# Two layers of a transformer with modulation on one core: Modulation's sums two products later in a pair with a third buffer, four places for context results, drains by copies, and a fixed order for the keys of layer 1

## The chip, the cores and the metric

The kernel runs on one core of a Trainium2 chip. A core has TensorE (PE, matmuls, with its weight loads PEld), VectorE (DVE), ScalarE (ACT), GpSimd (POOL), and a queue SP from which transfers between the chip's memory and the core's are issued, in order. [...] The metric is device time in microseconds, from one launch.

## The reference, cut to what matters

```python
for layer in range(2):                       # D = 1024, 1024 latent and 256 context positions
    mod_l = (silu(c) @ ada_w[layer] + ada_b[layer]).reshape(batch, 1, 6, D)
    mod_c = (silu(c_ctx) @ ada_w[layer] + ada_b[layer]).reshape(1, 1, 6, D)
    h_l = modulate(x, norm1_g[layer], mod_l, 0)       # rms_norm(x) * (1 + scale) + shift
    h_c = modulate(ctx, norm1_g[layer], mod_c, 0)
    y_c, y_l = ab_mixer(...) if layer == 0 else c_mixer(...)
    x = x + mod_l[:, :, 2] * y_l
    x = x + mod_l[:, :, 5] * mlp(modulate(x, norm2_g[layer], mod_l, 3))   # square(relu(h @ w1)) @ w2
    if layer == 0:
        ctx = ctx + mod_c[:, :, 2] * y_c
        ctx = ctx + mod_c[:, :, 5] * mlp(modulate(ctx, norm2_g[layer], mod_c, 3))
return x
```

The mixer of layer 0 joins a recurrent part with gates and an attention over a window; that of layer 1 is a full attention of 8 query heads over 2 heads of keys and values, whose queries and keys are normalised and rotated. The hidden width of the feed-forward part (mlp) is 4096.

## The kernel before

Data lie transposed: 128 features on the partitions, positions along a row. Each float32 operand is split in a high part and the rest (ACT copies the high part, POOL or DVE subtracts), and a product is three matmuls: high by high, high by rest, rest by high.

The feed-forward part handles the latent positions in two groups of 512 and the weights in blocks of 2 x 2, and gets their four products from seven (sums of operands are multiplied, results are sums of products). `mlp_hidden` goes through 16 pairs of hidden blocks (pairs 0 and 1 in `start`, the rest in `pair(b, A, nxt)`). A pair is seven products of 12 matmuls of 512 columns (`prod`, all at L569): 11 by B11, S1 by T1, 12 by B21, S2 by T2, 22 by T4, S3 by T3, S4 by B22. In layer 0 come 48 matmuls of 256 columns for the context (`direct`), 24 behind the third product and 24 behind the sixth. Banks 0 to 6 take products in turn, bank 7 what fills in. DVE adds the products up in temporaries of the tag "u" (`temp()`, L623), ten places in turn; ACT squares (`finish`, L581 and L582), SP stores the results. At the end of a pair stand the column sums (`column_sums`), in the next one behind S1 the row sums (`row_sums`). Two of the later pairs also do the sums of pairs 0 and 1 (`late_load`).

`filler` puts Modulation of layer 1 in layer 0's pairs: 12 blocks of 512 columns (`ada_sums`). A block has eight loads of 128 x 512 numbers (tag "raw", L202), which DVE multiplies by a number per partition and adds up (L209 the first, L211 the others), for blocks 0 to 3 in two streams (latent, context; the second stream in two halves), for the rest in one. Then matmuls by ones (L220) add over the partitions, and DVE copies the result with the bias (L223). The accumulators have one place each, so the next block begins when L220 is done. In `pair`, `fill` takes one of three steps of a block at three places: loads and updates 0 to 3, loads and updates 4 to 7, L220 and L223.

`mlp_out` then multiplies by the second weights, again in seven products (m1 to m7), two at a time in banks 0 to 3 and 4 to 7, over the hidden blocks. At the end of a group of products `drain` adds the four banks to x: directly by DVE (L1002), or by an ACT copy into a buffer "y" (L1013) and a later addition from there (`flush`). Splits of the next operands (L378 on ACT, L379 on DVE) run beside it.

Layer 1's keys and values (`keys`, `vals`) and the first queries (`project`) follow. A key's squares (L441, L447) are added over the partitions by a matmul with ones (L475), the queries' by L1812. In the attention DVE folds the maxima of a block of scores (L1842, L1845), PE transposes them (L1869); POOL subtracts in `weigh` (L1907). At its end the other mixer outputs are split (`split_mix`, L379) and multiplied (`out`).

The order of instructions on each engine is set by a scheduler that goes by priority, which is the order of the code, and by what waits for what; inside `manual_schedule` it is that of the code. Matmuls of `pair` are written out in the code's order, and DVE's instructions of sums are put where buffers and priority allow.

## Time and profile before

| | |
|---|---|
| median of 3 runs | 2917.3 us (2915.07 to 2924.1) |
| profiled execution | 2912.01 us, span 2910.2 us |
| mean granted clock of TensorE | 0.977 of full speed |
| busy: PE, DVE, ACT, POOL | 2753.9, 1994.1, 1497.0, 1145.2 us |
| loads and stores | 432.10 MB, 148 GB/s over the span |

The span is from the first to the last instruction of the profiled execution; its time as a run has 1.8 us beside it. [...] Busy PE at a clock of 0.50 counts as busy.

### The profile page before, as it was taken

Reading aid. Unit: us, or ns where it says so; the run is one execution under the profiler, and the core shown is the slowest. Engines: PE = TensorE matmul, PEld = TensorE weight load, DVE = VectorE, ACT = ScalarE, POOL = GpSimd, SP = SyncE. Lnnn points to the kernel's source line nnn. Section 1 sums busy time; section 2 is a strip of 40 time slices with the busy share of each in tenths; the row PEclk is TensorE's granted clock in tenths of the full one; section 3 lists DMA queues with packets and bytes.
Section 4 is the critical chain, followed back from the end, with each engine's and each line's share of the span. In section 5 each row is a group of like instructions: output and inputs, shape, how many; then the busy total and the mean of one; then the engine's idle time right before and its main releaser. Section 6 shows DMA issues by size and latency. Waiting matters only on the chain.

```text
span 2910.2 us, 41857 instructions
## 1 busy us (share of the span) xinstructions
PE 2753.9 (95%) x15174; PEld 2344.9 (81%) x15174; DVE 1994.1 (69%) x3296; ACT 1497.0 (51%) x2628; POOL 1145.2 (39%) x757
## 2 busy tenths in 40 slices
PE   6799999999999999999999998999989999999999
PEld 3678788878787777778878897999987888888877
DVE  5836555667867876766777845888886567756665
ACT  5655554444654233343435645888875555544332
POOL 3431220110227455560000653777765298840000
PEclk9999999999999998999999999999999999999999
DMA  6213233352324456569764740000017245577664
GB/s 229 60 49 102 78 101 130 120 194 73 121 84 141 151 188 202 187 225 346 245 215 151 255 151 30 21 25 26 19 62 229 88 140 196 192 250 275 214 228 146
DMA packets 200367, 432.10 MB, mean 148 GB/s; under 512 B 21216, under 2 KB 46944, under 8 KB 200160
## 3 DMA queue, kind: packets, MB, share of 16 engines
q1 hardware_dynamic: 200160, 429.43, 44.4%
q8 instruction: 119, 1.95, 0.3%
q14 instruction: 88, 0.72, 0.1%
HBM read 326.85 MB, written 102.50 MB: 148 GB/s over the span
## 4 chain that ended last, share of the span: by engine, by line
PE 62%; DVE 9%; DMA 6%; issue 6%; POOL 3%; ACT 3%; SPq 0%; DVEq 0%; POOLq 0%; ACTq 0%
PE psum L569 15%; PE psum L997 15%; PE psum L404 4%; PE psum L406 4%; PE psum L405 4%; PE psum L1895 4%; DMA hhiraw<-in_w 3%; PE psum L2080 3%; PE psum L1801 3%; PE psum L1090 2%; POOL W L379 2%; DVE W L379 2%; DMA F<-in_ada_w 1%; PE psum L1421 1%; DVE F L623 1%
## 5 line engine op out<-in xcount | busy, mean ns | idle before, releaser
L379 POOL TENSOR_TENSOR W<-F,W 128x512 fp32r<-128x512 f32 (+2 forms) x323 | 513.5, 1606 | 560.7 <-ACT W L378 435.5
L997 PE MATMUL psum<-W,W 128*128 128x512 f32 x2688 | 617.4, 391 | 11.3 <-DVE x L1002 8.2
L997 PEld LDWEIGHTS psum<-W,W 128*128 128x128 f32 x2688 | 506.2, 189 | 122.0 <-DVE x L1002 9.0
L569 PE MATMUL psum<-hhi,W 128*128 128x512 f32 (+1 forms) x1600 | 442.8, 358 | 9.6 <-ACT F L581 8.7
L378 ACT ACTIVATE W<-F 128x512 fp32r<-128x512 f32 (+2 forms) x380 | 274.7, 738 | 257.4 <-POOL F L542 103.4
L569 PEld LDWEIGHTS psum<-hhi,W 128*128 128x128 f32 x1600 | 287.3, 190 | 55.7 <-ACT F L581 9.7
L569 PE MATMUL psum<-hlo,W 128*128 128x512 f32 (+1 forms) x800 | 286.0, 357 | 0.0
L378 ACT ACTIVATE W<-hhiraw 128x1024 fp32r<-128x1024 f32 x98 | 104.0, 1062 | 331.9 <-PE psum L997 252.8
L404 PE MATMUL psum<-hhi,W 128*128 128x512 f32 (+1 forms) x624 | 232.2, 372 | 2.6 <-ACT F L179 1.4
L406 PE MATMUL psum<-hhi,W 128*128 128x512 f32 (+1 forms) x624 | 228.5, 366 | 1.3 <-POOL W L379 1.3
L405 PE MATMUL psum<-hlo,W 128*128 128x512 f32 (+1 forms) x624 | 228.0, 365 | 0.0
L923 DVE TENSOR_TENSOR hhiraw<-hhiraw 128x512 f32<-128x512 f32 x154 | 105.0, 688 | 125.1 <-DMA hhiraw<-in_w 124.1
L372 POOL TENSOR_TENSOR hlo<-F,hhi 128x512 fp32r<-128x512 f32 (+1 forms) x28 | 35.0, 1254 | 359.0 <-ACT F L371 354.2
L542 POOL TENSOR_TENSOR F<-F 128x512 f32<-128x512 f32 x112 | 169.4, 1513 | 9.9 <-DMA F<-in_w 2.6
L569 PEld LDWEIGHTS psum<-hlo,W 128*128 128x128 f32 x800 | 152.5, 191 | 22.3 <-issue 0.2
L379 DVE TENSOR_TENSOR W<-hhiraw,W 128x1024 fp32r<-128x1024 f32 x98 | 119.5, 1220 | 48.6 <-ACT W L378 48.6
L404 PEld LDWEIGHTS psum<-hhi,W 128*128 128x128 f32 x624 | 118.7, 190 | 25.0 <-ACT F L1353 2.8
L581 ACT ACTIVATE F<-F 128x512 f32<-128x512 f32 x84 | 52.5, 625 | 161.4 <-DVE F L623 161.3
L406 PEld LDWEIGHTS psum<-hhi,W 128*128 128x128 f32 x624 | 118.4, 190 | 20.3 <-POOL W L379 1.7
L405 PEld LDWEIGHTS psum<-hlo,W 128*128 128x128 f32 x624 | 118.9, 191 | 16.7 <-issue 1.4
L569 PE MATMUL psum<-x,W 128*128 128x512 f32 x504 | 123.7, 389 | 0.0
L379 DVE TENSOR_TENSOR W<-hloraw,W 128x1024 fp32r<-128x1024 f32 x98 | 119.3, 1218 | 0.0
(426 smaller groups left out, 6540.7 us busy)
## 6 DMA issues: line engine op xcount, KB each, us to landing
F<-in_w SPq DMA_DIRECT2D x104, 512.0 KB, 4.3
hloraw<-hd SPq DMA_DIRECT2D x90, 512.0 KB, 4.8
hd<-F SPq DMA_DIRECT2D x144, 256.0 KB, 2.2
hhiraw<-in_w SPq DMA_DIRECT2D x72, 512.0 KB, 3.9
hhiraw<-in_w SPq DMA_DIRECT2D x116, 256.0 KB, 5.1
F<-in_ada_w SPq DMA_DIRECT2D x96, 256.0 KB, 3.0
hd<-x SPq DMA_DIRECT2D x88, 256.0 KB, 2.3
F<-in_win SPq DMA_DIRECT2D x33, 512.0 KB, 3.7
```

The costliest lines, as they stand in the source:

```text
L378: nc.scalar.activation(hi, src, AF.Copy)
L379: eng.tensor_tensor(lo, src, hi.bitcast(F32), op=ALU.subtract)
L404: nc.tensor.matmul(ps, sh, mh, start=i == 0, stop=False)
L405: nc.tensor.matmul(ps, sh, ml, start=False, stop=False)
L406: nc.tensor.matmul(ps, sl, mh, start=False, stop=i == n - 1)
L542: add = lambda o, p, q, how: nc.gpsimd.tensor_tensor(o, p, q, op=how)
L569: nc.tensor.matmul(ps, w[i][:, p], B[j][k], start=first and j == 0 and m == 0, stop=last and j == 3 and m == 2)
L923: tt = lambda o, p, q, how: eng.tensor_tensor(o, p, q, op=how)
L997: nc.tensor.matmul(bank(base + i), A[u][:, p], B[v], start=first and m == 0, stop=last and m == 2)
L1801: nc.tensor.matmul(ps, s[:, c], m[:, j, t0 : t0 + QT], start=j == 0 and i == 0, stop=j == ND - 1 and i == 2)
L1895: nc.tensor.matmul(u.o[:, :QT], v[x], p[y], start=c == 0 and m == 0, stop=c == 2 * NB - 1 and m == 2)
L2080: self.nc.tensor.matmul(ps, x[:, c], y, start=first and m == 0, stop=last and m == 2)
```

## The change

Seven edits. In `pair`, the step with L220 stands behind the third product instead of behind the first, and the three steps begin one pair earlier; `fp` gets a third place "raw", taken from the places "u" in layer 0. In `start`, `direct` puts the context's results into the four places "kept" instead of the one place "uc". In `mlp_out`, products with a single use (m6, m7) are drained by copies, except in the last group; the second row of the context's products takes banks 0, 2, 5, 6 instead of 3, 4, 5, 6. Layer 1's keys become one generator for each head, with two buffers for the squares, additions and splits of latent keys on POOL, in an order written out, with the values' chunks between. At the end of attention three splits move from DVE to POOL. In `qk_first` (layer 0) a multiplication by the rotation's cosines stands behind the squares and copies.

```diff
@@ qk_first
-        nc.vector.tensor_tensor(t[:, :n], ps[:, :n], gc[:, l0 : l0 + n], op=ALU.mult)
         nc.scalar.activation(sq[:, :n], ps[:, :n], AF.Square)
...
+        nc.vector.tensor_tensor(t[:, :n], ps[:, :n], gc[:, l0 : l0 + n], op=ALU.mult)
@@ mlp_hidden
+        kept, rest = (cuts(F, H, *(o + i * H for i in range(n))) for o, n in ((3 * PG, 4), (7 * PG, 2)))
         fp = Area()
-        fp.place("raw", cuts(F, H, 5 * PG + H, 6 * PG))
+        fp.place("raw", cuts(F, H, 5 * PG + H, 6 * PG) + (rest[1:] if ctx else []))
...
-            finish(ps, tp.tile([P, CTX], F32, tag="uc"), hc[b][:, e * CTX : e * CTX + CTX])
+            finish(ps, tp.tile([P, CTX], F32, tag=tag), hc[b][:, e * CTX : e * CTX + CTX])
...
-                        direct(f, A[f // 2][2 * (f % 2) : 2 * (f % 2) + 2], g)
+                        direct(f, A[f // 2][2 * (f % 2) : 2 * (f % 2) + 2], g, "kept")
...
-            tp.place("u", kept + rest + [c for t in spare for c in cuts(t, H, 0, H)])
+            tp.place("u", kept + rest[: 1 if ctx else 2] + [c for t in spare for c in cuts(t, H, 0, H)])
@@ pair
-            def fill(last=False):
-                if filler and b > 2 + last:
+            def fill(k):
+
+                if filler and b > k:
                     next(filler(fp, psp, "N"), None)
...
-            fill(True)
             step()
             ps = bank()
             prod(ps, A["S1"], T1)
...
             prod(ps, A["12"], B21)
+            fill(2)
             tt(h11, ps, t)
             finish(h11, h11, part(b, 5))
+            fill(1)
             for g in ctx:
                 direct(f0, (A["11"], A["12"]), g)
-            fill()
...
             tt(t, t, ps, ALU.subtract)
-            fill()
+            fill(1)
@@ mlp_out
-                        drain(base, to[m], final or len(to[m]) == 1, now, done.get(m, ()))
+                        drain(base, to[m], final, now, done.get(m, ()))
...
-        for row, banks in enumerate(((4, 5, 6, 7), (3, 4, 5, 6))):
+        for row, banks in enumerate(((4, 5, 6, 7), (0, 2, 5, 6))):
@@ layer 1
+        def keys(g, kv):
...
+            ps = self.proj(psp, "A", wk[kv], t0, n)
+            yield
+            tile = lambda tag, bufs=1: kp[kv].tile([P, H], F32, tag=tag, bufs=bufs)[:, :n]
+            sq = tile("qsq", 2)
+            nc.scalar.activation(sq, ps[:, :n], AF.Square)
...
+                nc.gpsimd.tensor_tensor(t, t, sw, op=ALU.add)
+            yield
+            ss = psp.tile("Q")
+            nc.tensor.matmul(ss[:, :n], self.ones, sq, start=True, stop=True)
...
+            self.split(*K, rs, nc.vector if vv else nc.gpsimd)
+            yield
...
+        with self.tc.manual_schedule(engines=engines):
+            for x in ks[0]:
+                next(x)
+            for g in range(1, 3):
+                for kv in range(NKV):
+                    next(ks[g][kv])
+                    next(ks[g - 1][kv])
+                    next(ks[g][kv])
+            vals(TGS[1], (0,))
+            next(ks[2][0])
+            vals(TGS[1], (1,))
+            next(ks[2][1])
...
-                    split_mix(CTX, j, stage[j])
+                    split_mix(CTX, j, stage[j], nc.gpsimd)
...
+        with self.tc.manual_schedule(engines=engines):
+            load_q(0)
+            vals(TGS[1], (2, 3))
+            load_q(1)
+            for k in range(2):
+                st = project(k)
+                run(st, 9)
+                vals(TGS[2], (k,))
+                run(st, 99)
```

Where instructions stand, on PE in the pair loop, at a block of sums with one stream. Before, L220 (ones by the accumulator F) stands between the first product and S1 (operands hidA and hb):

```order
L569 MATMUL psum<-hlo,W_4615 128x512
L569 MATMUL psum<-hhi,W_4615 128x512
L220 MATMUL psum<-ones,F 128x2 x4
L569 MATMUL psum<-hidA,W_4615 128x512
L569 MATMUL psum<-hb,W_4615 128x512
L569 MATMUL psum<-hidA,W_4615 128x512 x2
L569 MATMUL psum<-hb,W_4615 128x512
```

In the changed kernel, at the end of the third product and the first matmuls of the context:

```order
L569 MATMUL psum<-hhi,W_4614 128x512
L569 MATMUL psum<-hlo,W_4614 128x512
L569 MATMUL psum<-hhi,W_4614 128x512 x2
L569 MATMUL psum<-hlo,W_4614 128x512
L569 MATMUL psum<-hhi,W_4614 128x512 x2
L569 MATMUL psum<-hlo,W_4614 128x512
L569 MATMUL psum<-hhi,W_4614 128x512 x2
L569 MATMUL psum<-hlo,W_4614 128x512
L569 MATMUL psum<-hhi,W_4614 128x512
L220 MATMUL psum<-ones,F 128x2 x4
L569 MATMUL psum<-hhi,W_4612 128x256
```

L220 moved behind S1 and behind the product of 12 by B21.

On DVE in the same loop, between the last update of one block with two streams and the start of the next (L623 are the pair's additions, a psum among the operands is a product being taken up). Before:

```order
L623 TENSOR_TENSOR F<-psum,F 128x512
L623 TENSOR_TENSOR x_7148<-psum,F 128x512
L623 TENSOR_TENSOR x_7149<-F,x_7148 128x512
L623 TENSOR_TENSOR x_7149<-x_7148 128x512
L623 TENSOR_TENSOR F<-F,x_7148 128x512
L623 TENSOR_TENSOR F<-psum,F 128x512
L623 TENSOR_TENSOR F<-F,x_7148 128x512
L223 TENSOR_TENSOR mod_81<-psum,vec 128x4 x2
L623 TENSOR_TENSOR F<-x_7148,F 128x512
L209 TENSOR_SCALAR F<-F,cs 128x512
L209 TENSOR_SCALAR x_7148<-F,cs 128x256
L209 TENSOR_SCALAR x_7149<-F,cs 128x256
```

In the changed kernel:

```order
L623 TENSOR_TENSOR F<-psum,x_7149 128x512
L623 TENSOR_TENSOR F<-x_7148,F 128x512
L623 TENSOR_TENSOR x_7149<-psum,x_7149 128x512
L623 TENSOR_TENSOR F<-F 128x512
L623 TENSOR_TENSOR x_7148<-x_7148,F 128x512
L623 TENSOR_TENSOR x_7148<-x_7149,F 128x512
L623 TENSOR_TENSOR x_7148<-psum,F 128x512
L623 TENSOR_TENSOR x_7149<-F,x_7149 128x512
L209 TENSOR_SCALAR F<-F,cs 128x512
L223 TENSOR_TENSOR mod_81<-psum,vec 128x4 x2
L209 TENSOR_SCALAR x_7148<-F,cs 128x256
L209 TENSOR_SCALAR x_7149<-F,cs 128x256
```

The same kind of additions stand between two blocks; L223 now stands behind the first operation of the block, and the two operations for the second stream behind it.

In the queue SP, at a block with one stream in pair 7 (L202 loads Modulation's weights, L534 those of the pairs, L584 stores squares: hd of the third product, hc of the context; L605 loads for the late sums). Before:

```order
L202 DMA F<-in_ada_w 128x512 x2
L605 DMA F<-hd_0_6496 128x512
L202 DMA F<-in_ada_w 128x512 x2
L584 DMA hd_7_6503<-x_7148 128x512
L202 DMA F<-in_ada_w 128x512
L584 DMA hc_7_6519<-F 128x256
L202 DMA F<-in_ada_w 128x512
L534 DMA F<-in_w 128x1024
L202 DMA F<-in_ada_w 128x512 x2
L534 DMA F<-in_w 128x1024
```

In the changed kernel:

```order
L202 DMA F<-in_ada_w 128x512 x2
L584 DMA hd_7_6503<-F 128x512
L202 DMA F<-in_ada_w 128x512
L584 DMA hc_7_6519<-F 128x256
L202 DMA F<-in_ada_w 128x512 x2
L534 DMA F<-in_w 128x1024
L202 DMA F<-in_ada_w 128x512 x3
L534 DMA F<-in_w 128x1024
```

Before, five of the eight loads stood ahead of the store of hc_7; now it is three, and three instead of two stand behind the first L534.

On PE at the keys of the context, layer 1 (L1801 a values' chunk, L475 the sums of squares). Before:

```order
L1801 MATMUL psum<-hhi,W_4614 128x256
L475 MATMUL psum<-F,ones 128x256
L1801 MATMUL psum<-hhi,W_4614 128x256
L1801 MATMUL psum<-hlo,W_4614 128x256
L1801 MATMUL psum<-hhi,W_4614 128x256 x2
L1801 MATMUL psum<-hlo,W_4614 128x256
L1801 MATMUL psum<-hhi,W_4614 128x256
L475 MATMUL psum<-F,ones 128x256
L1801 MATMUL psum<-hhi,W_4614 128x256
```

In the changed kernel (L1741 the sum of squares, L404 to L406 the values' chunks):

```order
L404 MATMUL psum<-W_104,hhi 128x256
L405 MATMUL psum<-W_104,hhi 128x256
L406 MATMUL psum<-W_104,hlo 128x256
L404 MATMUL psum<-W_103,hhi 128x256
L1741 MATMUL psum<-F,ones 128x256
L404 MATMUL psum<-W_103,hhi 128x256
L405 MATMUL psum<-W_103,hhi 128x256
L406 MATMUL psum<-W_103,hlo 128x256
```

The two sums of squares stood 7 matmuls apart, in one chunk; now they stand 43 matmuls apart (the other isn't shown), among chunks of values for latent positions.

## Rows read from the trace of the kernel before

**Rows 1.** The page, part 1: engines, busy time, share of the span, instructions.

```profile
PE 2753.9 (95%) x15174; PEld 2344.9 (81%) x15174; DVE 1994.1 (69%) x3296; ACT 1497.0 (51%) x2628; POOL 1145.2 (39%) x757
```

**Rows 2.** Waits of PE, whole span: us in total, times, longest us.

```profile
PE psum L220 <- DVE F L211: 29.4, 8, 7.1
...
PE psum L1205 <- ACT x L1193: 8.1, 1, 8.1
```

**Rows 3.** Windows: us, busy time of each engine, granted clock, DMA share, GB/s.

```profile
966.00:1002.80 36.80, 30.02 (x149) 25.91 (x150) 28.32 (x41) 12.23 (x25) 18.06 (x13) 0.87 0.46 152
...
912.10:1276.70 364.60, 335.20 (x1713) 288.12 (x1711) 264.28 (x322) 128.96 (x250) 212.31 (x144) 0.93 0.55 181
```

**Rows 4.** Timeline of DVE, pairs 4 and 5: start, us, engine, line, operation.

```profile
963.95 0.88 DVE L211 SCALAR_TENSOR_TENSOR x<-F,cs,x 128x256 f32<-128x256 f32 x2
...
973.80 1.17 DVE L623 TENSOR_TENSOR F<-F,x 128x512 f32<-128x512 f32 x1 [3.81 <-ACT F L582]
...
976.60 1.51 DVE L209 TENSOR_SCALAR F<-F,cs 128x512 f32<-128x512 f32 x1
...
999.27 0.87 DVE L211 SCALAR_TENSOR_TENSOR x<-F,cs,x 128x256 f32<-128x256 f32 x2
```

**Rows 5.** Groups of DVE by form, 912.1 to 1276.7: busy us, mean ns.

```profile
L211 DVE SCALAR_TENSOR_TENSOR F<-F,cs 128x512 f32<-128x512 f32 x78 | 72.4, 928 | 42.1 <-DMA F<-in_ada_w 41.8
...
L623 DVE TENSOR_TENSOR F<-psum,F 128x512 f32<-128x512 f32 x43 | 28.6, 679 | 0.5
...
L623 DVE TENSOR_TENSOR F<-F 128x512 f32<-128x512 f32 x20 | 26.2, 1312 | 2.5 <-ACT F L582 2.4
```

**Rows 6.** Waits of DVE, 1035.9 to 1276.7 (pairs with one stream).

```profile
DVE F L211 <- DMA F<-in_ada_w: 33.8, 35, 2.0
```

**Rows 7.** Waits of the queue SP, 870 to 1040.

```profile
SPq L202 <- DVE x L211: 39.2, 22, 3.7
```

**Rows 8.** The page, part 6: DMA issues, KB each, median us to landing.

```profile
F<-in_ada_w SPq DMA_DIRECT2D x96, 256.0 KB, 3.0
...
hd<-F SPq DMA_DIRECT2D x144, 256.0 KB, 2.2
```

**Rows 9.** Timeline of PE at five waits: the bracket names wait and releaser.

```profile
895.50 0.39 PE L569 MATMUL psum<-hhi,W 128*128 128x256 f32 x1 [1.79 <-ACT F L581]
...
1483.19 7.11 PE L997 MATMUL psum<-W,W 128*128 128x512 f32 x20 [4.12 <-DVE x L1002]
...
1669.41 1.82 PE L1090 MATMUL psum<-hb,W 128*128 128x256 f32 x13 [1.65 <-DVE x L1097]
...
2176.62 0.41 PE L1869 MATMUL psum<-ident,F 128*128 128x128 f32 x2 [3.93 <-DVE F L1845]
...
2819.49 6.75 PE L997 MATMUL psum<-W,W 128*128 128x512 f32 x22 [4.06 <-DVE x L1002]
```

**Rows 10.** Timeline of DVE before two of these waits.

```profile
1481.26 1.22 DVE L379 TENSOR_TENSOR W<-hloraw,W 128x1024 fp32r<-128x1024 f32 x1
...
1482.39 2.72 DVE L1002 SCALAR_TENSOR_TENSOR x<-psum,mod,x 128x512 f32<-128x512 f32 x4
...
2168.52 3.10 DVE L379 TENSOR_TENSOR hlo<-F,hhi 128x512 fp32r<-128x512 f32 x3 [0.65 <-ACT hhi L378]
...
2174.77 1.71 DVE L1845 TENSOR_TENSOR F<-F 128x256 f32<-128x256 f32 x1
```

**Rows 11.** Timeline of POOL, end of attention.

```profile
2166.90 2.96 POOL L1907 TENSOR_TENSOR W<-x,W 128x1280 fp32r<-128x1280 f32 x1 [2.17 <-ACT x L1906]
2173.31 2.89 POOL L1907 TENSOR_TENSOR x<-x,x 128x1280 fp32r<-128x1280 f32 x1 [3.45 <-ACT x L1906]
```

**Rows 12.** Waits of PE, 1730 to 1806 (keys and first queries, layer 1).

```profile
PE psum L475 <- ACT F L441: 3.3, 2, 2.5
PE psum L1812 <- ACT F L1809: 3.2, 2, 1.9
PE psum L475 <- ACT F L447: 3.0, 2, 2.8
```

More of the change, by code (lines that the diff above doesn't have):

```diff
@@ L509, in mlp_hidden @@
         tp.place("s", cuts(F, H, 5 * PG))
+        kept, rest = (cuts(F, H, *(o + i * H for i in range(n))) for o, n in ((3 * PG, 4), (7 * PG, 2)))
         fp = Area()
-        fp.place("raw", cuts(F, H, 5 * PG + H, 6 * PG))
+        fp.place("raw", cuts(F, H, 5 * PG + H, 6 * PG) + (rest[1:] if ctx else []))
         fp.place("acc0", cuts(F, H, 6 * PG + H))
-        kept, rest = (cuts(F, H, *(o + i * H for i in range(n))) for o, n in ((3 * PG, 4), (7 * PG, 2)))
         tp.place("kept", kept)
@@ L1748, in vals @@
                 self.split(*V, ps[:, :256], nc.vector)
-        ks = [keys(g) for g in TGS]
+        ks = [[keys(g, kv) for kv in range(NKV)] for g in TGS]
         for _ in range(ND):
             next(side)
-        next(ks[0])
+        for x in ks[0]:
+            next(x)
         next(side)
-        vals(TGS[0])
+        vals(TGS[0], range(4))
         for _ in side:
@@ L1761, in mixer1 @@
         VC = vc[:, :PG].rearrange("p (s c d) -> p s c d", s=2, c=2)
-        next(ks[0])
-        next(ks[1])
-        next(ks[2])
-        next(ks[1])
-        next(ks[2])
+        E = mybir.EngineType
+        engines = {E.PE, E.DVE, E.Activation, E.Pool}
+        with self.tc.manual_schedule(engines=engines):
+            for x in ks[0]:
+                next(x)
+            for g in range(1, 3):
[7 more added lines that the diff above has]
+            next(ks[2][1])
         qtab = self.rope_tables(self.area(PG, 3 * PG), a["rope1"], V_CQ, V_CQS, "rt")
@@ L1925, in load_mix, with split_mix @@
             nc.sync.dma_start(m, mixd[j][:, t0 - CTX : t0 - CTX + 512])
-        def split_mix(t0, j, m):
-            self.split(self.hhi[:, j, t0 : t0 + 512], self.hlo[:, j, t0 : t0 + 512], m, nc.vector)
+        def split_mix(t0, j, m, eng=nc.vector):
+            self.split(self.hhi[:, j, t0 : t0 + 512], self.hlo[:, j, t0 : t0 + 512], m, eng)
         raw = cuts(self.F, PG, 0, PG)
@@ L1986, in early @@
                 out(3, range(ND))
-        for h in range(2):
-            load_q(h)
-        for k in range(2):
-            vals(TGS[1 + k])
-            run(project(k), 99)
+        with self.tc.manual_schedule(engines=engines):
[7 more added lines that the diff above has]
+                run(st, 99)
         psp = self.banks(A=(0,), O=(1,), S=(3, 4, 5, 6, 7))
         ACC, S = (self.psum[:, b * 512 : e * 512] for b, e in ((2, 3), (3, 8)))
-        E = mybir.EngineType
         us = {}
@@ L2002, in on @@
                 f(us[k], *a)
-        with self.tc.manual_schedule(engines={E.PE, E.DVE, E.Activation, E.Pool}):
+        with self.tc.manual_schedule(engines=engines):
             for k in range(NU + 2):
```

27 lines of the change are left out of this document (17 added, 10 removed).

## Prediction

> **What bounds the kernel now.** TensorE (PE) works for 2753.9 of the 2910.2 us of the span [rows 1]; so I read the waits of PE, the largest first, then the stretch of each. The largest is that of the matmuls at L220, which add up Modulation's sums over the partitions, for VectorE's (DVE's) last update at L211: 29.4 us in 8 waits [rows 2], all in the pair loop of layer 0. From the product S1 of pair 3 to that of pair 15 are 12 pairs in 364.6 us, with PE at a mean granted clock of 0.93 [rows 3]; 7% of 364.6 is 25.5 us lost to stretches at the lower level. Waits and clock make 54.9 us; without both a pair would take (364.6 - 54.9) / 12 = 25.8 us. The loop loses 25.5 / 29.4 = 0.87 us to the clock for each us of wait; I use that ratio below.
>
> Why PE waits there is seen on DVE [rows 4]. The last update of one block of sums ends at 963.95 + 0.88 = 964.83; the first operation of the next (L209) starts at 976.60, 11.8 us later, because the pair's other additions stand between, one of which waits 3.81 us for ScalarE (ACT). The block then lasts until 999.27 + 0.87 = 1000.14, 23.5 us. One round on DVE is 35.3 us where PE needs 25.8; in the pair of 966.0 to 1002.8 DVE is busy 28.32 of 36.80 [rows 3], so most of it is work, not waiting. Blocks 0 to 3 carry two streams (24 operations), blocks 4 to 11 one stream (8). In the pairs of the latter DVE waits 33.8 us in 35 waits for the loads of Modulation's weights [rows 6].
>
> **The sums.** The change removes none of them. It moves L220 of a block behind two more products, starts the blocks one pair earlier, and gives their loads a third buffer, whose place it takes from the temporaries (nine instead of ten). A pair holds 84 matmuls of 512 columns and 48 of 256, as much as 108 of 512, so a product of 12 is 25.8 x 12 / 108 = 2.9 us, and the move gives 5.7 us of cover, once. On DVE the order now is: the additions of the pair, the copy L223, then the block with only four or five additions in it.
> Two-stream rounds: the block falls from 23.5 to some 22.5 us, no more, since in SP's queue the stores of the pair's first results, which wait for ACT, still stand among its loads; of the 11.8 us between blocks I keep 11, since the additions that wait for squares stay. That is 33.5 us against 26.7 for PE (25.8 and the 8 matmuls of L220, some 0.9). Block 0 is done beside pair 2; block 1 starts in step with PE, 1 us behind its L220, and is 26.7 - 23.5 = 3.2 us early; block 2 comes 33.5 - 26.7 - 3.2 = 3.6 us late, block 3 another 6.8: 10.4 us.
> One-stream rounds: a load lands in 3.0 us [rows 8] and an update takes 0.93 [rows 5]. With two buffers there is one update each (3.0 + 0.93) / 2 = 2.0 us, 16 us a block; with three 1.3 us, 10.5, and I add 2 for the stores among the loads. With 11 between, a round falls from 27 to 23.5, under 25.8, so PE should wait no more, but for two pairs that do the sums of the first two pairs as well: five additions of 1.31 us [rows 5], 6.5 us, of which the 2.3 to spare in this and the pair before take up 4.6. Some 2 us each, 4 in all.
> So 14.4 us of waits stay, with the clock 14.4 x 1.87 = 27: the gain is 54.9 - 27 = **28**. Bounds: 5 us of waits left give 45.5, 20 give 17.5.
>
> **Drains by copies.** At the change from the second to the third group of output products of layer 0, PE waits 4.12 us for DVE [rows 9], which reaches the four drains only at 1482.39, behind other work [rows 10]; ACT copies now free the banks. That would give 4.12 x 1.87 = 7.7. But the split that ends at 1481.26 + 1.22 = 1482.48 [rows 10] makes an operand of the next step, which PE would reach 12 matmuls (2.7 us) after the drain that it no longer waits for, at 1479.07 + 2.7 = 1481.8: 0.7 us of wait, and about as much at the following step, since the four additions now stand ahead of its split. So **5.5** (4 to 7.7). In layer 1 the like wait is 4.06 us [rows 9]; there the splits come earlier: **5** (4 to 7.6).
>
> **Keys of layer 1.** Of the waits in this stretch [rows 12], 3.3 and 3.0 us are of the sum of squares for ACT and 3.2 of the queries' for ACT, of which the shorter, 1.3, stays. In the new order at least 24 matmuls of 512 or 48 of 256 columns stand between a key's projection and its sum of squares, 5.7 us that cover the activations. Taken away: 9.5 - 1.3 = 8.2, and some clock: **9** (4 to 14 with the clock's ratio on all; below if POOL, which takes the additions and splits, comes late for the first scores).
>
> **End of attention.** PE waits 3.93 us [rows 9] for L1845 on DVE, ahead of which three subtractions take 3.10 [rows 10]. They go to GpSimd (POOL). There 128x1280 takes 2.96 us and ends at 2169.86 [rows 11], so 128x512 takes some 1.2, and three end at 2173.4. PE's three outputs that need them now end at 2176.62 - 3.93 = 2172.69, 1.07 us behind DVE's subtractions (2168.52 + 3.10); then near 2174.5, 2.1 us before L1845's result is taken up now: **2** (-0.5 to 5.5).
> The low end comes from this. L1845 reads two operands in SBUF, took 1.71 us, and ended at 2176.48 [rows 10], just after POOL's operation had ended at 2176.20 [rows 11]; an addition with one operand in PSUM takes 0.68 us, with both in SBUF 1.31 in the mean [rows 5].
> [...]
> I take 2 because DVE, freed of 3.10 us, should issue L1845 before POOL starts that operation.
>
> **The rest.** Four places for the context's results take away a wait of 1.79 us [rows 9] but not those beside it: **1** (0 to 3). Other banks for the context's second row take away 1.65 us [rows 9], unless the first keys wait for bank 0: **1.5** (0 to 2). In layer 0 the multiplication moved behind the squares changes the order of many instructions near a wait of 8.1 us for the gates [rows 2]; it may come earlier or later: **0** (-5 to 5).
>
> **Sum.** 28 + 5.5 + 5 + 9 + 2 + 1 + 1.5 = 52 us. The durations are of one execution of 2912.0 us, 5.3 below the median of the three runs, 2917.3; taken from the median the sum gives **2865**.
>
> **Rivals.**
> The loop's waits go altogether: the rounds on DVE get so short that two-stream blocks keep pace. For it: DVE waits 3.81 us in a round for ACT [rows 4], which could vanish when DVE runs late. Against it: 28.32 us of work [rows 3] where PE needs 26.7. Gain of the loop 50, 22 more: **2843**.
> The third buffer does nothing: SP issues all transfers in one order, and its loads already wait 39.2 us in 22 waits for DVE [rows 7]; if other waits in the queue hold the load of the third buffer as well, rounds stay at 35.3 and 27 us. Then block 1 is 26.7 - 24.5 = 2.2 us early, blocks 2 and 3 come 6.4 and 8.6 late, and eight one-stream rounds (27 for 26.2, with the 4 matmuls of L220) wait 0.8 each: 21.4 us, with the clock 40. The loop gains 15, 13 less: **2878**. For it speaks the queue's order: in pair 7 three of the eight loads now stand ahead of the context's store, before it was five. Against it: PE needs the block two products later too, and waits only if that, too, is used up.
> Slower: the place that the loads take away. With nine places for temporaries, the third result of a pair (h11) goes where the pair before had v, which the row sums have just rewritten and SP must store: a store lands in 2.2 us [rows 8]. Between stand L223 and four updates, some 5 us on DVE in a one-stream pair. DVE, and then PE, waits only if the store goes out 2.8 us late; it stands in the queue near loads that wait up to 3.7 us each [rows 7]. At x us a pair over 13 pairs beyond what the round has to spare, the loop changes by 13x - 54.9, and the rest gains 24; it is slower by 0.3% (8.8 us) from x = 6.7 on, at 7 us **2929**. Against it: that takes four such waits in a row, in each pair.
>
> **How the numbers follow.** 0.3% (9 us) is about what a measurement tells from no change. My forecast: 0.52. All waits of the loop gone: 0.17. Third buffer idle: 0.2. Slower: 0.03. The remaining 0.08 are cases in which another edit costs some 20 us of the gain (the start of layer 0, the keys): from 2885 on, or with the buffer idle within 0.3%. The likeliest alone spans 2852 to 2876; 2841 to 2889 reaches over the first two rivals and the lower bound of the loop's gain, 17.5, with that of other terms, and leaves out 0.15. Faster by over 0.3%: 0.95, within: 0.02, slower: 0.03.
>
> **What would show it.** Waits of L220 below 15 us and a clock of 0.96 or more in the loop, in the pairs of blocks 2 and 3 and in the two with the late sums, would show the sums right; waits at all pairs, the idle buffer; waits of DVE for a store, the slower case. No wait over 1.5 us for L1003 (the former L1002) shows the drains, none over 1 us at the keys' sums of squares the order of the keys, L1845 ending before 2175 the end of attention. The forecast is wrong if PE waits elsewhere for what DVE, now denser, does later, above all for its drains of the banks in pairs 2 to 5.

## The result, and the profile after

The changed kernel takes 2882.4 us (2880.9 to 2886.6, four executions) where the kernel before took 2916.2 (2913.8 to 2924.1) beside it: ratio 0.9882, 95% interval 0.9860 to 0.9904. That is 34 us gained where 52 were forecast. The profiled execution has a span of 2881.0 us, 29.2 less than before.

The page's busy times show that the work is the same [rows 1]; PE does its 15174 matmuls in 8.6 us less because less of them falls into stretches at a granted clock of 0.50 (69 us where it was 96, by windows of 2 us that are at 0.50 throughout; mean granted clock 0.981, before 0.977):

```profile
PE 2745.3 (95%) x15174; PEld 2334.7 (81%) x15174; DVE 1992.4 (69%) x3285; ACT 1503.1 (52%) x2640; POOL 1160.9 (40%) x768
```

The waits of PE, as in [rows 2] (us in total, times, longest). L220 fell from 29.4 us to 7.4; a new line is the output products' (L998):

```profile
PE psum L220 <- DVE F L211: 7.4, 5, 3.8
...
PE psum L998 <- DVE W L379: 6.4, 13, 0.9
...
PE psum L1830 <- DVE F L1744: 4.6, 1, 4.6
...
PE psum L998 <- ACT W L378: 2.9, 1, 2.9
...
PE psum L1927 <- DVE F L1892: 2.9, 1, 2.9
```

The windows of the 12 pairs of [rows 3], from S1 of pair 3 to S1 of pair 15, and of the beginning of the output products (us, busy times, granted clock, DMA share, GB/s):

```profile
902.90:1242.40 339.50, 323.47 (x1714) 279.30 (x1713) 263.84 (x324) 130.46 (x254) 215.79 (x145) 0.97 0.59 194
```

```profile
1262.00:1290.00 28.00, 20.24 (x63) 15.09 (x62) 11.71 (x13) 10.86 (x18) 12.61 (x5) 0.76 0.69 236
```

So the loop gained 25.1 us (364.6 to 339.5), its clock rose from 0.93 to 0.97. But in the 28 us behind it PE is busy for 20.2, at a clock of 0.76. The timeline of PE there shows four waits:

```profile
1267.62 0.51 PE L998 MATMUL psum<-W,W 128*128 128x512 f32 x1 [2.94 <-ACT W L378]
1270.06 5.96 PE L998 MATMUL psum<-W,W 128*128 128x512 f32 x14 [1.94 <-POOL W L379]
1277.70 0.96 PE L998 MATMUL psum<-W,W 128*128 128x512 f32 x3 [1.67 <-ACT F L581]
1279.86 5.49 PE L998 MATMUL psum<-W,W 128*128 128x512 f32 x12 [1.21 <-DVE x L623]
```

These are 7.8 us of waits, and 24% of 28 us, 6.7, lost to the clock: from 1280 to 1284 us, at 0.50, PE does 10 of these matmuls, from 1286 to 1290, at 1.00, 20. The kernel before had two short ones there, 0.38 and 1.22 us, with a clock of 1.00 over the first 28 us of its output products:

```profile
1302.93 0.98 PE L997 MATMUL psum<-W,W 128*128 128x512 f32 x3 [0.38 <-ACT F L581]
```

Followed back (releaser by releaser), the last two of the four are for the last pair's results (L581 is ACT's relu in `finish`, L623 DVE's additions), and the first two for splits of operands (L378 on ACT, L379 on POOL) that stand in ACT's order behind such a relu, which waits for DVE:

```profile
1265.33 0.63 ACT L581 ACTIVATE x<-x 128x512 f32<-128x512 f32 x1 [14.63 <-DVE x L623]
```

So the four lead, in part through ACT's and POOL's order, to DVE, which waits, in pair 15, for stores:

```profile
1255.65 2.46 DVE L623 TENSOR_TENSOR x<-x,F 128x512 f32<-128x512 f32 x1 [9.54 <-DMA hd<-x]
...
1264.60 1.89 DVE L623 TENSOR_TENSOR x<-psum,x 128x512 f32<-128x512 f32 x3 [5.17 <-DMA hd<-x]
```

Both, which write places of the temporaries, wait for a store that still reads there, 9.54 and 5.17 us. The queue SP shows why the first store (hd<-x, issued at 1251.80) is late: loads of the output stage (L881) stand ahead of it and of the stores before it,

```profile
1241.66 7.88 SPq L881 DMA_DIRECT2D F<-in_w  x3
1249.65 0.37 SPq L599 DMA_DIRECT2D hd<-F  x1
...
1251.80 0.40 SPq L599 DMA_DIRECT2D hd<-x  x1
...
1258.14 1.05 SPq L599 DMA_DIRECT2D hd<-x  x2
```

and those loads wait for POOL's splits to free their buffers (SP's waits from 1238 to 1262):

```profile
SPq L881 <- POOL W L379: 12.4, 6, 5.9
```

The stores of the second wait were not held up: they go out at 1258.14, as the addition that began at 1255.65 ends, and DVE goes on 6 us later. That wait is the landing of a store just issued, in a ring that comes back to its place too soon.

Two stretches tell most of what follows, for all kernels of this study. They are differences of start times in the timeline of PE: **loop** from the first S1, in `start`, to S1 of pair 15 (before: 834.9 to 1276.7), **behind** from there to the context's first matmul in the output stage (L1091; before: 1614.3), which holds the last pair and the latent output products with the drains.

| kernel | median us | loop | behind |
|---|---|---|---|
| before | 2916.2 | 441.8 | 337.6 |
| after | 2882.4 | 411.1 | 347.5 |
| after, again | 2876.5 | 409.4 | 345.7 |
| sums and third buffer alone | 2894.6 | 409.7 | 346.2 |
| after without third buffer | 2882.5 | 426.0 | 332.8 |
| third buffer alone | 2904.0 | 420.7 | 346.9 |
| drains alone | 2908.2 | 442.4 | 335.3 |
| after, tenth place given back | 2873.5 | 408.6 | 341.1 |
| after, squares ahead | 2876.5 | 411.7 | 342.3 |
| both | 2872.0 | 409.7 | 339.1 |
| both, loads by GpSimd | 2881.9 | 413.0 | 344.2 |
| both, keys' split on VectorE | 2869.7 | 409.2 | 340.2 |
| the last, place given back earlier | 2871.5 | 416.2 | 333.6 |

The medians come from several chips; that of the kernel before, measured beside each, was between 2913.9 and 2916.2. The changed kernel's stretches differ by 2 us between its two profiles and its medians by 6. Up to the keys of layer 1 the kernel with the squares ahead has the same code, so the stretch behind scatters by 5 us (342.3 to 347.5, mean 345.2); "tenth place given back", "both" and "both, keys' split on VectorE" are likewise one code up to there (339.1 to 341.1, mean 340.1).

### The profile page after: what moved, and what is told of

Its sections match the earlier page's. It is cut to its first block, busy times and chain, and to the rows that moved or that the text cites. A ratio compares the mean times of both kernels' runs of the same rounds, so it can differ in the third digit from the quotient of the medians.

```text
span 2881.0 us, 41902 instructions
## 1 busy us (share of the span) xinstructions
PE 2745.3 (95%) x15174; PEld 2334.7 (81%) x15174; DVE 1992.4 (69%) x3285; ACT 1503.1 (52%) x2640; POOL 1160.9 (40%) x768
## 4 chain that ended last, share of the span: by engine, by line
PE 55%; DVE 12%; DMA 8%; issue 7%; ACT 4%; POOL 4%; SPq 0%; DVEq 0%; POOLq 0%; ACTq 0%
PE psum L998 12%; PE psum L569 12%; DMA hhiraw<-in_w 4%; PE psum L406 4%; PE psum L404 4%; PE psum L405 4%; PE psum L1924 4%; PE psum L2112 3%; PE psum L1830 3%; DVE W L379 3%; POOL W L379 2%; DVE F L623 1%; DVE F L211 1%; PE psum L1091 1%; DVE x L1003 1%
## 5 line engine op out<-in xcount | busy, mean ns | idle before, releaser
L379 POOL TENSOR_TENSOR W<-F,W 128x512 fp32r<-128x512 f32 (+2 forms) x323 | 516.5, 1614 | 524.9 <-ACT W L378 398.3
L998 PE MATMUL psum<-W,W 128*128 128x512 f32 x2688 | 622.7, 393 | 14.5 <-DVE W L379 6.4
L998 PEld LDWEIGHTS psum<-W,W 128*128 128x128 f32 x2688 | 506.5, 189 | 130.4 <-DVE W L379 15.8
L378 ACT ACTIVATE W<-F 128x512 fp32r<-128x512 f32 (+2 forms) x380 | 273.7, 739 | 250.7 <-POOL F L542 98.4
L378 ACT ACTIVATE W<-hhiraw 128x1024 fp32r<-128x1024 f32 x98 | 103.9, 1061 | 326.3 <-PE psum L998 252.6
L404 PE MATMUL psum<-hhi,W 128*128 128x512 f32 (+1 forms) x624 | 233.0, 373 | 6.6 <-DVE F L478 6.6
L406 PE MATMUL psum<-hhi,W 128*128 128x512 f32 (+1 forms) x624 | 228.1, 366 | 1.3 <-POOL W L379 1.3
L542 POOL TENSOR_TENSOR F<-F 128x512 f32<-128x512 f32 x112 | 170.2, 1520 | 17.4 <-DMA F<-in_w 10.3
L379 DVE TENSOR_TENSOR W<-hhiraw,W 128x1024 fp32r<-128x1024 f32 x98 | 119.6, 1221 | 46.2 <-ACT W L378 46.1
L404 PEld LDWEIGHTS psum<-hhi,W 128*128 128x128 f32 x624 | 119.2, 191 | 27.4 <-DVE F L478 7.0
L406 PEld LDWEIGHTS psum<-hhi,W 128*128 128x128 f32 x624 | 118.9, 191 | 18.6 <-POOL W L379 1.7
L581 ACT ACTIVATE F<-F 128x512 f32<-128x512 f32 x82 | 51.3, 626 | 134.9 <-DVE F L623 134.9
L379 DVE TENSOR_TENSOR W<-hloraw,W 128x1024 fp32r<-128x1024 f32 x98 | 119.4, 1219 | 0.1
```

The source lines that it names most:

```text
L378: nc.scalar.activation(hi, src, AF.Copy)
L379: eng.tensor_tensor(lo, src, hi.bitcast(F32), op=ALU.subtract)
L404: nc.tensor.matmul(ps, sh, mh, start=i == 0, stop=False)
L406: nc.tensor.matmul(ps, sl, mh, start=False, stop=i == n - 1)
L542: add = lambda o, p, q, how: nc.gpsimd.tensor_tensor(o, p, q, op=how)
L998: nc.tensor.matmul(bank(base + i), A[u][:, p], B[v], start=first and m == 0, stop=last and m == 2)
```

## The experiments

**The theory** after these rows: the third buffer and the move of the sums bring what was forecast in the loop, but the place that the buffer takes from the temporaries costs some 14 us at the loop's end, where the stores stand in SP's queue behind waiting loads. **The rival**: the third buffer does little, the move does the work, and what is lost behind the loop comes from other edits (the drains, the changed order).

### The sums alone, and the third buffer taken out

The first has the diff of `pair` and of the buffer alone, the second is the changed kernel with

```diff
-            fp.place("raw", cuts(F, H, 5 * PG + H, 6 * PG) + (rest[1:] if ctx else []))
+            fp.place("raw", cuts(F, H, 5 * PG + H, 6 * PG))
...
-            tp.place("u", kept + rest[: 1 if ctx else 2] + [c for t in spare for c in cuts(t, H, 0, H)])
+            tp.place("u", kept + rest + [c for t in spare for c in cuts(t, H, 0, H)])
```

> The kernel before with the edits of Modulation's sums alone (L220 two products later, blocks one pair earlier, third buffer, nine temporaries). If the edits are independent, the loop gains what it gained in the whole change (25 us from S1 of pair 3 to S1 of pair 15, and some 4 in pair 2), and loses again what the whole change lost behind the loop (3 us up to the first output product, 13 in the first steps of the output stage): 2916 - 13 = 2903, and the waits behind the loop are there. If these came from another edit (drains, context places), they are absent here and the time is near 2887.

> The changed kernel without the third buffer: two buffers for the loads, ten temporaries; L220 stays two products later. Theory A (the nine places make DVE wait for stores, in the loop 15 us of DVE's time, behind the loop 15 us at one go): no wait of DVE for a store of hd, the 16 us behind the loop come back, the loop changes by less than 6: 2866 to 2872. Theory B (the loads need three buffers, the waits behind the loop come from operands that are late for a loop that has become faster): the loop loses 13 us or more, the waits behind it stay: 2893 or more.

Measured beside the same executions of the kernel before (median 2914.6): the sums alone 2894.6 (ratio 0.9935, 0.9916 to 0.9955), between the two times expected (2903 and 2887), without the third buffer 2882.5 (0.9894, 0.9877 to 0.9910), between theory A (2866 to 2872) and theory B (2893 or more): the waits behind the loop went as in A, the loop lost as in B. The sums alone show the loop of the changed kernel (409.7) and also its loss behind (346.2), so the loss comes with the sums' edits, not with the drains or the keys. Without the third buffer L220 waits as before,

```profile
PE psum L220 <- DVE F L211: 28.1, 4, 8.2
```

the loop is 15.8 us and not 30.7 shorter than before, and the output products begin without any wait:

```profile
1280.26 20.11 PE L998 MATMUL psum<-W,W 128*128 128x512 f32 x88
```

No DVE wait for a store is left there. So the third buffer gives 15 us in the loop (426.0 to 411.1) and takes 15 behind it (332.8 to 347.5); by the second run of the changed kernel it is 17 and 13, with a median 6 us lower, so with or without it the kernel takes the same time within the scatter.

### The third buffer alone

The kernel before with the diff's lines on `fp` and "u" and nothing else.

> The kernel before with the third buffer and the nine temporaries alone, Modulation's sums where they were. By the prediction's rival that it was the late loads that held the loop, the buffer alone takes most of the loop's gain: the loop from the fourth pair to the last 364.6 to about 347 us, the kernel about 2890 us. My reading after the changed kernel and the one without the third buffer: the buffer alone is worth about 15 us in the loop and gives 12 to 15 back at the beginning of the output products, where VectorE stands for stores of hidden sums: 2912 us (2906 to 2916), with the waits for the copies and splits of the hidden rows at that place.

2904.0 us (0.9959, 0.9944 to 0.9974), 8 less than I expected; the forecast's rival (2890) misses by more, on the other side. Behind the loop the loss is 9.3 us (346.9 against 337.6 before, both without the drains' edit), less than the 12 to 15 expected. Its pair 14 is slow (30.9 us from S1 to S1), and yet DVE waits 5.29 and 5.42 us for stores in pair 15; without the third buffer pairs 13 and 14 take 25.7 us each, and it doesn't wait. So the loss goes with the missing place and not with the pace at which PE reaches the loop's end. In the loop it gained 21.1 us and not 15: the two edits overlap, since 15.8 (the move, in the kernel without the buffer, which has the context places too) and 21.1 (the buffer alone) give 30.7 together and not 36.9.

### The tenth place given back for the last pairs

The blocks of Modulation are nearly done in pair 14; the place then returns to the temporaries.

```diff
+            if ctx and b == NFF // 2 - 2:
+                u, i = tp.tags["u"]
+                tp.place("u", rest[1:] + [u[(i + j) % len(u)] for j in range(len(u))])
             ps, t = bank(), temp()
```

> The changed kernel, with the third buffer's place given back to the temporaries at the start of pair 14, when the last load of Modulation's weights has been used. Theory A: the loop up to pair 14 stays as it is, DVE's waits of 9.5 and 5.2 us for stores in pair 15 vanish, and with them the 16 us behind the loop: 2867. Theory B (late operands of the output stage): no change within 3 us, 2882.

2873.5 us (0.9864, 0.9846 to 0.9883). The loop stayed (408.6), the stretch behind fell to 341.1. DVE's waits for stores from 1240 to 1290, first of the changed kernel, then of this one:

```profile
DVE x L623 <- DMA hd<-x: 14.7, 2, 9.5
```

```profile
DVE x L623 <- DMA hd<-x: 3.2, 1, 3.2
DVE F L623 <- DMA hd<-F: 3.1, 1, 3.1
```

and the output products begin at once, with two waits instead of four:

```profile
1263.90 3.56 PE L1001 MATMUL psum<-W,W 128*128 128x512 f32 x15
1270.43 1.65 PE L1001 MATMUL psum<-W,W 128*128 128x512 f32 x3 [2.97 <-ACT F L581]
1272.59 13.77 PE L1001 MATMUL psum<-W,W 128*128 128x512 f32 x50 [0.51 <-DVE x L623]
```

Behind the loop 5 us are recovered, in the mean of the three profiles with the place given back (340.1) and the three without (345.2), of the 12 that the latter lie above the kernel without the third buffer (332.8). That the rest is the same mechanism, 6.3 us of waits being left, was still open.

### The keys' squares ahead

The second suspect is the keys of layer 1, which gained little: PE waits 2.87 us for a key's sum of squares,

```profile
1735.60 1.49 PE L1741 MATMUL psum<-F,ones 128*128 128x512 f32 x2 [2.87 <-ACT F L1730]
```

because in ACT's fixed order the square (L1730) stands behind the split of the key before (L378 to hidA), which waits for DVE's end of that key's norm (L1746):

```profile
1734.43 0.63 ACT L378 ACTIVATE hidA<-F 128x512 fp32r<-128x512 f32 x1 [4.45 <-DVE F L1746]
1734.97 0.58 ACT L1730 ACTIVATE F<-psum 128x512 f32<-128x512 f32 x1
```

The edit puts the square of the next key ahead of it; the rotation's copies stay behind (a yield more in `keys`, and one more `next` in the order).

```diff
             nc.scalar.activation(sq, ps[:, :n], AF.Square)
+            yield
...
             for x in ks[0]:
                 next(x)
+                next(x)
             for g in range(1, 3):
                 for kv in range(NKV):
                     next(ks[g][kv])
+                    next(ks[g][kv])
                     next(ks[g - 1][kv])
```

> The changed kernel with the square of each latent or context key of layer 1 ahead of the preceding key's chain in ACT's order (the rotation's copies stay behind it). If the square stands late because ACT waits for that chain, the wait of 2.9 us of the sum of squares for ACT vanishes and the one of 4.6 us for DVE behind it shrinks, 5 to 9 us with the clock: 2875. If DVE's chain, stretched beside POOL's additions and splits, is the limit anyway, the wait only moves: 2880 to 2882.

2876.5 us (0.9873, 0.9857 to 0.9889). The wait for the square is gone, but the next one took its place: the sum of squares now waits for its bank, which DVE (L465) frees late.

```profile
1735.94 0.77 PE L1742 MATMUL psum<-F,ones 128*128 128x256 f32 x1 [3.85 <-DVE F L465]
```

From the context rows to the first values product of the attention it takes 198.9 us, the changed kernel 198.3 and 200.2. The waits of PE from 1715 to 1815 are 10.0 us, in the changed kernel 10.0 and 11.6. Whatever the median shows, the edit gained nothing in its own place: the waits for the square became waits for DVE.

### The drains alone, both mends, and the changed kernel again

`drains_only` is the kernel before with the line `drain(base, to[m], final, now, ...)`; `both` holds the two mends above.

> The kernel before with one edit alone: the output products' last blocks drain through copies in both layers. By the prediction it gains 5.5 us in layer 0 and 5 us in layer 1, so about 2904 us against about 2914.5 of the kernel before on the same chip. By the stretches of the kernels that already hold the edit (layer 0's output stage 315.3 to 310.6 us in the kernel without the third buffer, layer 1's 313.1 to between 308.7 and 311.7) it gains 4.7 and 1.4 to 4.4 us, about 2907 us. If the copies only move the wait to the hi and lo splits behind them on VectorE, it gains nothing: 2914 us.

> The changed kernel with both mends together: the tenth place given back for the last two pairs, and the squares of the keys issued ahead of the preceding hi split. If each mend is worth what it showed alone (9 and 6 us), 2868 us. If the second mend is worth nothing in its own stretch (keys to the first values product 97.8 before it and 98.1 with it, so its 6 us lay in other stretches and are the scatter between runs), as the ring alone: 2873 us (2870 to 2876).

> The changed kernel once more, beside the others on one chip, as their measure. If executions on different chips compare within their scatter: 2881 us (2878 to 2885), the ring's mend then 8 us and the squares' mend 4 to 5 us below it. If the earlier run of it fell high by chance: 2876 us, and the squares' mend is worth nothing.

Before is 2913.9 here. The drains alone: 2908.2 (0.9978, 0.9968 to 0.9989), 5.7 us, as expected from the stretches. The 4.12 us wait of layer 0 [rows 9] has become one of DVE's split,

```profile
1482.45 9.73 PE L997 MATMUL psum<-W,W 128*128 128x512 f32 x41 [0.45 <-DVE W L379]
```

and from 1480 to 1520 there are three such waits:

```profile
PE psum L997 <- DVE W L379: 1.8, 3, 0.7
```

Both mends: 2872.0 (0.9846, 0.9830 to 0.9863), the same as the ring's alone: the squares are worth nothing. The changed kernel again: 2876.5 (0.9865, 0.9850 to 0.9881), 5.9 below its first run; so the two mends are worth 4.5 us on one chip, about the scatter of the medians; the stretches behind the loop show 5.0 in the mean.

### Loads of the output stage by GpSimd

If the store is late because waiting loads stand ahead of it in SP's queue, the loads may go elsewhere (`now[0]` holds the step whose loads are issued).

```diff
-            nc.sync.dma_start(t if len(src.shape) == 2 else ...)
+            eng = nc.gpsimd if hc and now[0] < 3 else nc.sync
+            eng.dma_start(t if len(src.shape) == 2 else ...)
```

> The kernel with both mends, and the loads of the first three steps of the output stage issued by GpSimd instead of SyncE. In the last two pairs SyncE's queue waits 14.6 us for GpSimd's splits in front of such loads, and the stores of hidden sums stand behind them. If that order is what still delays VectorE at the loop's end (3.1 and 3.2 us of waits for stores) and with it the first output products (3.0 us and a stretch at half clock), the stretch from the last pair to the context rows falls from 339 to about 333 us and the kernel from 2872 to about 2866 us. Rival: VectorE is late there by its own work or the landing of the stores, and nothing changes: 2872 us. Rival: nine more issues on GpSimd delay its splits for the sums' products, and the last two pairs get longer: 2875 us or more.

2881.9 us (0.9885, 0.9871 to 0.9900), 10 more than the kernel without the edit took on another chip (2872.0): the third case by the time. POOL now issues these loads in its own order, eight of the nine 0.30 to 0.42 us behind a split of its own that they waited for, and it then waits for loads to land (waits of POOL, 1197 to 1290):

```profile
POOL F L932 <- DMA F<-in_w: 10.7, 3, 4.1
```

DVE still waited 7.25 us for a store. Its queue shows why: the load of the step behind the three was still SP's, stood 11.1 us for POOL's split, and the store went out behind it:

```profile
SPq L885 <- POOL W L379: 11.1, 1, 11.1
```

```profile
1264.18 0.38 SPq L885 DMA_DIRECT2D F<-in_w  x1
1264.62 0.98 SPq L599 DMA_DIRECT2D hd<-x  x2
```

The output products waited longer than in any other kernel:

```profile
1279.45 1.65 PE L1006 MATMUL psum<-W,W 128*128 128x512 f32 x3 [7.08 <-ACT F L581]
```

So the order in SP's queue does delay a store, here with a single load left in it; what it costs alone stays open, since the edit left that load and made POOL wait for the others.

### The keys' lo split on VectorE

The last keys' wait leads to DVE's chain of a key's norm, in which single steps take two and a half to four times as long beside POOL. Rows of the changed kernel, first DVE, then POOL (hb<-F,hidA is a key's lo split):

```profile
1728.54 1.77 DVE L464 TENSOR_TENSOR F<-F 128x512 f32<-128x512 f32 x1 [0.78 <-ACT F L461]
...
1730.35 0.69 DVE L465 SCALAR_TENSOR_TENSOR F<-psum,F 128x512 f32<-128x512 f32 x1
1731.08 1.80 DVE L466 TENSOR_SCALAR F<-F 128x512 f32<-128x512 f32 x1
...
1740.79 0.43 DVE L466 TENSOR_SCALAR F<-F 128x512 f32<-128x512 f32 x1
```

```profile
1725.41 1.28 POOL L379 TENSOR_TENSOR hb<-F,hidA 128x512 fp32r<-128x512 f32 x1 [11.52 <-ACT hidA L378]
...
1728.49 1.28 POOL L1738 TENSOR_TENSOR F<-F 128x512 f32<-128x512 f32 x1
1730.07 2.52 POOL L379 TENSOR_TENSOR W<-F,W 128x1024 fp32r<-128x1024 f32 x1 [0.30 <-ACT W L378]
```

```diff
-            self.split(*K, rs, nc.vector if vv else nc.gpsimd)
+            self.split(*K, rs, nc.vector)
```

> The kernel with both mends, the lo split of the keys of the grid rows moved from GpSimd to VectorE. If VectorE's chain for a key's norm is long because GpSimd works beside it (its 512-wide steps there took 2.12 and 1.49 us, elsewhere in the same stretch 0.43 and 0.69), the stretch from the context rows to the first values product falls from 96.8 to about 94.5 us and the wait for a key's sums of squares of 3.8 us shrinks to under 2: the kernel 2870 us. Rival: the four splits of 0.7 us each lengthen VectorE's own order by as much as they free: 97 to 98 us, the kernel 2872 us.

2869.7 us (0.9844, 0.9822 to 0.9866), 2.3 below `both`, which is within the scatter. The stretch from the end of the context rows to the first values product fell from 96.8 to 95.3 us (95.1 in the next kernel, which has the edit too; 97.9 and 98.1 in the other two kernels with the squares ahead and the split on POOL). The wait for the bank stayed at 3.8 us against my expectation; what shrank is a wait behind it, of L404 for L1748, from 1.7 to 0.5. The steps that were to get shorter did not: `both`, then this kernel,

```profile
1731.71 1.49 DVE L464 TENSOR_TENSOR F<-F 128x512 f32<-128x512 f32 x1 [1.05 <-ACT F L461]
```

```profile
1730.49 1.46 DVE L464 TENSOR_TENSOR F<-F 128x512 f32<-128x512 f32 x1 [1.05 <-ACT F L461]
```

and L466 went from 2.12 to 2.14. They stand beside the rotation's addition and a split of 128x1024 that isn't the keys', and both are still POOL's; the keys' lo split ended at 1726.69 in the rows above, before either step began. From the first to the last L464 of the keys it takes 36.0 us in both kernels. What was gained lies behind the last one, where the wait of L404 is: 29.8 us to the first values product in the two kernels with the edit, 31.3 in all three with the squares ahead and the split on POOL. So the direction was right, and the reason given for it was not; why that wait shrank stays open.

### The place given back one pair earlier

```diff
-            if ctx and b == NFF // 2 - 2:
+            if ctx and b == NFF // 2 - 3:
                 u, i = tp.tags["u"]
-                tp.place("u", rest[1:] + [u[(i + j) % len(u)] for j in range(len(u))])
+                tp.place("u", [u[(i + j) % len(u)] for j in range(len(u))] + rest[1:])
+                r, i = fp.tags["raw"]
+                fp.place("raw", [r[(i + j) % 3] for j in range(3) if (i + j) % 3 != 2])
```

> The kernel before this one (both mends, the keys' lo split on VectorE), with the tenth place given back for the last three pairs instead of two, at the ring's end, Modulation's loads then going through two buffers. If the ring is still what makes VectorE late at the loop's end, the stretch from the last pair to the context rows falls from 340 towards the 333 to 335 us that the kernels without the third buffer show, less up to 2 us that the loop loses with two buffers in one pair more: 2865 us. Rival: what is left there is VectorE's and ScalarE's own work on the last pair's hidden rows, and the ring has given what it can: 2870 us, the wait for the copies of those rows at the first output products about 3 us as before.

2871.5 us (0.9844, 0.9826 to 0.9862) against 2865 expected, the same as the kernel it starts from, but the stretches moved as the theory says: behind 340.2 to 333.6, the value without the third buffer (332.8), and from 1240 to 1290 DVE no longer waits for a store. The output products begin without a wait:

```profile
1273.83 16.48 PE L1003 MATMUL psum<-W,W 128*128 128x512 f32 x72
```

The loop gave the 7 us back, in pair 14 (35.8 us from S1 to S1 instead of 26.4), where Modulation's loads again had two buffers:

```profile
1228.44 1.87 PE L220 MATMUL psum<-ones,F 128*128 128x2 f32 x8 [5.60 <-DVE F L211]
```

A pair 14 that is 9 us longer also gives the stores time to land, so this run alone doesn't show that the whole loss behind the loop is the missing place. For that speak the pair of kernels above, a slow pair 14 with nine places and the loss (third buffer alone), fast pairs with ten and none (without third buffer).

## Why the prediction was right and wrong

The direction, the range and the mechanism of the largest term held; the sum was 18 us too high by the first run (15 by the second, 52 against 37.4), and the miss has one large cause, the place, and two smaller ones, the keys (9 too high with the context's second row) and the drains (5 too high).

- **The sums**, forecast 28: the loop's column shows 32.1 for the sums alone, all of it in the 12 pairs of the forecast, and 30.7 and 32.4 in the whole change; of the 30.7, 25.1 lie in the 12 pairs and 5.5 in pair 2. I had left 14.4 us of waits in the 12 pairs; there are 15.9. L220 waits 2.43, 0.69 and 3.75 us for blocks 1, 2 and 3 (forecast: none, 3.6 and 6.8), and the two pairs with late sums have a wait of 3.1 us each (forecast 2 each), not at L220 but at a product that waits for DVE; the second of them has 5.4 us of waits in all. The clock is 0.97.
- **The step that failed** is that the place taken for the third buffer had no term in the sum. I had named the mechanism in the slower rival, a store that goes out late behind waiting loads, and priced it only as a wait in every pair of the loop ("that takes four such waits in a row, in each pair"). In the pairs of the changed kernel DVE waits 1.1 to 3.0 us for a store, and PE little. It decides once, in the last pair: there the loads of the output stage, which wait for POOL, stand in the same queue, and PE has nothing else to do but what hangs on DVE. Price: 9 us by the kernels without the drains' edit (346.2 and 346.9 against 337.6), 10 to 15 by those with it (342.3 to 347.5 against 332.8). My closing sentence, that the forecast is wrong if PE waits elsewhere for what DVE does later, was the right one, at another place than I gave.
- **Third buffer idle** (2878) is nearest to the measured time, for another reason: the buffer works in the loop and is paid for behind it.
- **Drains**, forecast 5.5 and 5: alone 5.7 in all. In layer 0 2.3 by the stretch, in layer 1 3.0 (313.1 to 310.1; between 308.7 and 311.7 in the kernels with the edit). The waits of 4.12 and 4.06 us went, and none over 0.9 for L998 is left of them; the products wait for the splits behind them more often than I counted (6.4 us in 13 waits), in layer 1 as in layer 0.
- **Keys**, forecast 9, with the context's second row 1.5: together some 1.5 (199.6 to 201.3 us in the four kernels without these edits, 197.5 to 200.2 in the seven with them and the split on POOL). I counted the matmuls between a projection and its sum of squares, and not that a fixed order puts the square behind the split of the key before it, on ACT, and behind that DVE's chain of a key's norm, which is longer beside the additions given to POOL (L464 took 0.68 us in the kernel before and takes 1.77 here). The waits of PE in this stretch were 11.6 us before and are 10.0 and 11.6 in the two runs of the changed kernel; 4.6 of them are one new wait, of the first queries' projection (L1830) for the end of that chain (L1744). The second row waits 2.00 us for DVE as it waited 1.65 [rows 9]: nothing gained there.
- **End of attention**, forecast 2: 2.4 in the mean over kernels with and without it (391.2 and 393.6 from the first to the last values product; the ranges, 389.8 to 392.9 and 392.3 to 394.0, just overlap). L1874 ended at 2149.61, ahead of POOL's operation, as I had taken it, and took 0.78 us instead of 1.71 [rows 10]; the low end, -0.5, supposed that it would end only with a later operation of POOL, which no run shows of it. The wait of 3.93 us is gone, but one of 2.91 came 10 us later, behind a split on DVE:

```profile
2148.83 0.78 DVE L1874 TENSOR_TENSOR F<-F 128x256 f32<-128x256 f32 x1
...
2154.89 1.59 DVE L379 TENSOR_TENSOR hlo<-F,hhi 128x512 fp32r<-128x512 f32 x1
```

```profile
2150.29 2.92 POOL L1936 TENSOR_TENSOR x<-x,x 128x1280 fp32r<-128x1280 f32 x1 [0.96 <-ACT x L1935]
```

- **Context places**, forecast 1: pair 2 is 5.5 us shorter with them (31.5 to 26.0, from its S1 to that of pair 3), but the sums alone, without them, have as short a loop in all (409.7): what they give early is waited for again by L220. **Start of layer 0**, forecast 0: the first S1 comes at 833.1 to 834.9 us in the four kernels without the edit, at 830.6 to 835.5 in the nine with it.

What stays open is why two runs of the changed kernel differ by 6 us; the kernel before differs by 2.3 beside them, the ratios' intervals overlap, and the second profile has 1.7 us less in the loop, 1.8 less behind it and 3 less in the last output products, but 2 more each in the context rows with the keys and in the attention. The keys, the end of attention, the context places and the start of layer 0 were not run alone; their shares are read from stretches.

## What to carry to other kernels

A buffer that is taken from another ring has its price where that ring is tightest, which here was a change of stage and not the loop in which it was judged: look there for who stores what, and what stands ahead of the store in its queue. A wait that is taken away shows the next one behind it: count for each edit what then comes last, on every engine with a fixed order, before its whole wait is put into the sum. When two edits aim at one loss, their gains overlap (15.8 and 21.1 gave 30.7).

## What the runs showed of the hardware

Two operations of VectorE took longer beside one of GpSimd. In the rows above (changed kernel, keys), L464 took 1.77 us and ended at 1730.31, 0.54 us after GpSimd's operation (1729.77); with none beside it, it took 0.69 (1721.34). L466, which takes 0.43 us alone (1740.79), took 1.80 and ended at 1732.88, 0.29 after GpSimd's (1732.59). So each ended shortly after the other was done. L465 between them, with one operand in PSUM (psum in its row), took 0.69 us beside the same operation of GpSimd, as it did without one (1740.06). Why the two took longer and this one didn't, no run shows. Beside the rotation's addition and the split of 128x1024 on GpSimd, cheap as they look on an engine that is 40% busy, VectorE took 1.1 and 1.4 us more here; for the keys' own lo split no row shows that.

Waits went with a loss of clock: 7.8 us of waits and 6.7 lost to it at the beginning of the output products, 29.4 and 25.5 in the loop before, 15.9 and 10 in the changed one (3% of 339.5). It isn't a fixed price: the kernel before had 1.6 us of waits at the beginning of the output products and a clock of 1.00.
